# Attention in a two-layer block: two heads' values beside each other in the array, weight sums as strips of ones, queries for two pairs at a time

## The chip, the cores and the metric

The kernel runs on one core of a Trainium2 chip. A core has five engines that work side by side and meet through semaphores: TensorE (PE, matrix products, results in PSUM; its weight loads are listed apart as PEld), VectorE (DVE), ScalarE (ACT), GpSimd (POOL) and SyncE (SP, which here issues the transfers from memory). Each engine takes its instructions strictly in the order of the program. The metric is the device time of one execution in microseconds (us), lower is better.

## The reference

The reference is a block of two layers on 512 tokens of 1024 features, with 256 context tokens. Layer 0 mixes by Fourier and long convolution, layer 1 by attention with compressed queries and keys; each ends in a feed-forward network with a short convolution. The change lies in the attention of layer 1, of which this is the core (16 heads; a head has 64 plain and 32 rotated query features and 64 value features; keys are the 512 tokens and the 256 of the context):

```python
def _mla_queries(a_q, q_a_norm, w_uq, q_norm, rope):
    q = (_rms_norm(a_q, q_a_norm) @ w_uq).reshape(B, L, MLA_HEADS, QK_HEAD_DIM)
    q = _rms_norm(q, q_norm)
    ...
    s = jnp.einsum('bqhd,bkhd->bhqk', qblk, k, preferred_element_type=jnp.float32) * scale
    p = jax.nn.softmax(s, axis=-1).astype(v.dtype)
    return jnp.einsum('bhqk,bkhv->bqhv', p, v)
```

## The kernel before

Features lie on partitions and tokens along the free axis. Most products are done three times in float32r (`mm3`, lines 175 to 177): high part times high part, and the two cross terms with the low parts, which `hi` (line 150, ACT) and `lo` (line 155, DVE) split off. Products on plain fp32 operands are one call and appear as two records each.

The attention stage works on eight pairs of heads. It is written as small steps, each a function of a pair `p` and a few indices, and the text `ORDER` lists them with an offset: the loop runs through the list again and again, and a step with offset `o` is done for pair `it + o`. Inside `manual_schedule` this order is the order on PE, DVE, ACT and POOL. So it is a cyclic pipeline over pairs; steps that belong to only one pair (`only`) are left out in the other rounds. The steps, with the lines of their work:

- `QT` makes the queries of a pair (512 tokens x 192 features, 24 products of 192 columns, tile `k`), `SQ` squares them (ACT, L1521), `TB` and `TX` multiply by the rotation tables (DVE, L1526 and L1530), `RD` sums the squares (L1534).
- `UK` makes the pair's keys (tile `k`), `KSQ`, `KH`, `KL` square, copy and split them, `KS` sums the squares by twelve small records (L1557). `RT` takes the roots of queries and keys together: 13 small DVE instructions (L1562, L1563 and `rsqrt`, L184 to L193).
- `U` scales the queries (ACT, L1570), `TR` transposes them (PE, L1577), `QC` and `QL` copy and split them.
- `SC` makes the scores of head `a` with key tile `j` in one of three banks `s`: head 0 by `mm3`, head 1 by a fp32 product (L1597). `EV` brings them to `S`, scaled (ACT, L1605).
- `MA` to `MD` (DVE) and `AR` (POOL, L1623) find the maximum over the keys, `SU` subtracts it (DVE, L1627), `EX` takes the exponential (ACT, L1630).
- `VP` and `VE` make the values of all heads once, in `V`. There, for each pair, 64 columns of ones stand between the two heads' 64 value columns. `PW` (L1651) multiplies 128 columns of it, the values and the ones, by the weights of one head and one key tile: twelve fp32 products of full width a pair, in a bank `pv` for each head. Half of the result are the values, half are the sums of the weights, repeated over 64 rows.
- `TZ` (L1657) and `TO` (L1662) copy sums and values out (ACT, half the rows at a time), `RC` (L1666) takes the reciprocal of the sums over 256 columns twice, `DV` (L1680) divides, `OH` and `OL` split the result.
- `WO` are output products that belong to the next stage, of two of its eight row blocks; `WA`, `WD`, `XA`, `XD` load and split weights, the loads by SP.

A product in strips exists in this kernel too: in `gemv_pe` (L236, before the first layer) four products of 32 output columns each stand side by side in the array, in fp32 over 512 columns, each with its own moving operand.

## Time and profile before

| | us |
|---|---|
| median of 3 runs | 1598.99 (1595.99 to 1599.34) |
| the profiled execution | 1599.1 |
| its span | 1597.3 |
| PE busy in the span | 1561.7 |
| DVE busy | 1058.8 |
| ACT busy | 626.1 |
| POOL busy | 109.0 |

The span runs from the first to the last instruction of the profiled execution. Busy time of matmuls is modelled, since they are pipelined: the time between two starts says what one costs, not its own length. In the lines of the profile `L1651` is a line of the kernel, `pv<-S,V` names what is written from what, `x192` counts records, and the two numbers behind the bar are the total in us and the mean of one in ns; what follows is idle time before these instructions and what ended it. On the chain of waits a piece has its start, the time that it holds the chain, and its engine and line.

### The profile page before, as it was taken

How to read it: one execution, taken by the hardware profiler on the slowest of the kernel's cores; microseconds unless marked ns; L12 is line 12 of the kernel's file. 1: busy time of each engine (PE TensorE's matmuls, PEld its weight loads, DVE VectorE, ACT ScalarE, POOL GpSimd, SP SyncE). 2: the span in 40 equal slices, each digit the busy share in tenths (PEclk: the TensorE clock that was granted, in tenths of full speed). 3: DMA queues.
4: the chain of work that ended last, by engine and by line, in shares of the span. 5: the costliest groups of instructions: out<-in, count | busy, mean ns of one | idle time of the engine just before them, and what ended most of it. 6: DMA issues, size and time to landing. Idle time of an engine off the chain costs nothing.

```text
span 1597.3 us, 20872 instructions
## 1 busy us (share of the span) xinstructions
PE 1561.7 (98%) x8248; PEld 1291.2 (81%) x8248; DVE 1058.8 (66%) x1772; ACT 626.1 (39%) x909; POOL 109.0 (7%) x113
## 2 busy tenths in 40 slices
PE   7999999999999999999999999999999999999999
PEld 4787888888888888888888887566559888888887
DVE  5788969878986356653464577899987644344343
ACT  4451234434223113221132347898853432233231
POOL 0012135000000000000000000221210000000000
PEclk9999999999999999999999999999999999999999
DMA  9336412532543134431342310000033222222222
GB/s 351 107 115 211 175 48 87 185 119 107 184 151 140 64 135 158 166 111 66 113 168 82 111 50 1 14 11 14 0 110 141 93 93 96 103 93 96 102 80 92
DMA packets 54542, 173.36 MB, mean 109 GB/s; under 512 B 6187, under 2 KB 9453, under 8 KB 53421
## 3 DMA queue, kind: packets, MB, share of 16 engines
q1 hardware_dynamic: 54445, 172.03, 30.5%
q8 instruction: 65, 1.06, 0.3%
q14 instruction: 32, 0.26, 0.0%
HBM read 166.24 MB, written 5.77 MB: 108 GB/s over the span
## 4 chain that ended last, share of the span: by engine, by line
PE 79%; DVE 15%; ACT 2%; issue 2%; POOL 1%; DMA 1%; SPq 0%; POOLq 0%; DVEq 0%; ACTq 0%
PE mm L175 23%; PE mm L177 23%; PE mm L176 23%; PE pv L1651 2%; DVE junk L260 2%; DVE S L1627 2%; DVE wl L155 1%; PE s L1597 1%; DVE wr L1666 1%; DVE hl L330 1%; ACT wh L150 1%; PE ms L236 1%; PE mm L638 1%; DVE mx L1611 1%; DVE nt L325 0%
## 5 line engine op out<-in xcount | busy, mean ns | idle before, releaser
L150 ACT ACTIVATE wh<-wr 128x1024 fp32r<-128x1024 f32 (+1 forms) x192 | 198.3, 1035 | 548.2 <-PE mm L176 512.5
L175 PE MATMUL mm<-hh,wh 128*128 128x512 f32 (+1 forms) x872 | 339.9, 391 | 2.1 <-ACT hh L326 0.9
L176 PE MATMUL mm<-hl,wh 128*128 128x512 f32 (+1 forms) x872 | 338.4, 388 | 2.3 <-DVE hl L330 2.3
L177 PE MATMUL mm<-hh,wl 128*128 128x512 f32 (+1 forms) x872 | 338.2, 388 | 1.9 <-DVE wl L155 1.9
L155 DVE TENSOR_TENSOR wl<-wr,wh 128x1024 fp32r<-128x1024 f32 (+2 forms) x192 | 231.4, 1208 | 143.6 <-ACT wh L150 139.3
L177 PEld LDWEIGHTS mm<-hh,wl 128*128 128x128 f32 x872 | 165.2, 190 | 35.5 <-DVE wl L155 2.5
L175 PEld LDWEIGHTS mm<-hh,wh 128*128 128x128 f32 x872 | 165.2, 190 | 35.2 <-issue 2.9
L176 PEld LDWEIGHTS mm<-hl,wh 128*128 128x128 f32 x872 | 165.6, 190 | 32.6 <-DVE hl L330 3.5
L260 DVE SCALAR_TENSOR_TENSOR junk<-wr,sb 128x1024 bf16<-128x1024 f32 x128 | 156.1, 1220 | 47.3 <-DMA wr<-wmodT 47.1
L1171 DVE SCALAR_TENSOR_TENSOR xr<-mm,mod,xr 128x512 f32<-128x512 f32 (+1 forms) x100 | 61.8, 631 | 170.0 <-PE mm L177 169.7
L176 PE MATMUL mm<-hlc,wh 128*128 128x256 f32 (+1 forms) x488 | 137.6, 282 | 0.0
L175 PE MATMUL mm<-hhc,wh 128*128 128x256 f32 (+1 forms) x488 | 137.6, 282 | 0.0
L177 PE MATMUL mm<-hhc,wl 128*128 128x256 f32 (+1 forms) x488 | 137.4, 282 | 0.0
L176 PE MATMUL mm<-al,wh 128*128 128x512 f32 x328 | 127.8, 389 | 0.0
L177 PE MATMUL mm<-ah,wl 128*128 128x512 f32 x328 | 127.7, 389 | 0.0
L175 PE MATMUL mm<-ah,wh 128*128 128x512 f32 x328 | 127.7, 389 | 0.0
L1651 PE MATMUL pv<-S,V 128*128 128x512 f32 x192 | 93.9, 598 | 2.6 <-ACT S L1630 2.6
L175 PEld LDWEIGHTS mm<-hhc,wh 128*128 128x128 f32 x488 | 91.7, 188 | 3.9
L176 PEld LDWEIGHTS mm<-hlc,wh 128*128 128x128 f32 x488 | 91.7, 188 | 3.9
L177 PEld LDWEIGHTS mm<-hhc,wl 128*128 128x128 f32 x488 | 93.4, 191 | 0.0
L1214 DVE TENSOR_TENSOR fg<-fg,mm 128x768 f32<-128x768 f32 (+1 forms) x44 | 36.1, 821 | 76.4 <-PE mm L177 75.7
L1212 ACT ACTIVATE fg<-fg 128x768 f32<-128x768 f32 (+1 forms) x44 | 32.5, 739 | 123.9 <-DVE fg L395 94.4
(381 smaller groups left out, 2836.0 us busy)
## 6 DMA issues: line engine op xcount, KB each, us to landing
wr<-w_up SPq DMA_DIRECT2D x88, 512.0 KB, 3.2
wr<-wmodT SPq DMA_DIRECT2D x80, 512.0 KB, 3.2
wr<-w_dn SPq DMA_DIRECT2D x32, 512.0 KB, 3.1
wm<-wmod0a SPq DMA_DIRECT2D x8, 1024.0 KB, 9.7
wr<-w_in SPq DMA_DIRECT2D x16, 512.0 KB, 4.3
wr<-w_out SPq DMA_DIRECT2D x13, 512.0 KB, 3.7
wr<-w_dn SPq DMA_DIRECT2D x17, 384.0 KB, 2.9
wr<-w_o SPq DMA_DIRECT2D x11, 512.0 KB, 3.5
```

The costliest lines, as they stand in the source:

```text
L150: self.nc.scalar.activation(dst, src, AF.Copy)
L155: (eng or self.nc.vector).tensor_tensor(dst, src, hi.bitcast(F32), op=ALU.subtract)
L175: mmul(out, wh, xh, start=start, stop=False)
L176: mmul(out, wh, xl, start=False, stop=False)
L177: mmul(out, wl, xh, start=False, stop=stop)
L236: nc.tensor.matmul(ps[32 * q : 32 * q + 32, :], self.sT[:, kt, :], raw[:, 512 * kt : 512 * kt + 512], start=kt < 4, stop=kt >= 4, tile_pos ...
L260: nc.vector.scalar_tensor_tensor(junk, raw, 1.0, self.sb[:, j, :], op0=ALU.mult, op1=ALU.mult, accum_out=acc)
L1171: nc.vector.scalar_tensor_tensor(x[m][:, a2:b2], ps[:, a2 + o : b2 + o], mod[:, 8 * sec + m, c : c + 1], x[m][:, a2:b2], op0=ALU.mult, op1 ...
L1212: nc.scalar.activation(g[:, :n], g[:, :n], AF.Silu)
L1214: v.tensor_tensor(a[:, :n], g[:, :n], pss[1][:, :n], op=ALU.mult)
L1627: v.tensor_tensor(c.S[a][h], c.S[a][h], mb.to_broadcast([P, 3, T]), op=ALU.subtract)
L1651: nc.tensor.matmul(c.P[a], V[:, j, o : o + 128], c.S[a][j // 3][:, j % 3, :], start=j == 0, stop=j == 5)
```

## The change

The change rewrites the attention stage and nothing outside of it.

- Values: `V` holds 1024 columns without ones. `PW` for a key tile is two products of 64 columns, one for each head, placed by `tile_position` at columns 0 and 64 of the array; both heads share one bank.
- Weight sums: `ZS` sums the weights by products with 32 columns of ones, four of them (head, half of the key tiles) at columns 0, 32, 64 and 96 of the array, three steps a pair, in one bank. `ZT` transposes the bank in blocks of 32x32 on DVE, `ZM` adds the two halves of each head by a small fp32 product with a 0/1 matrix (`fold`), `ZR` takes the reciprocal of 16 columns, `ZB` spreads it by another transpose, `DV` multiplies the values straight out of PSUM. `TZ`, `TO` and `RC` go.
- Queries: `QT`, `SQ`, `TB`, `TX`, `RD` work on four heads and half of the tokens (products of 384 columns), and `RT` takes the roots of two pairs (40 columns); the first two pairs' roots are taken in two parts.
- Both heads keep the plain features on rows 0 to 63 and the rotated ones on 64 to 127, and the keys of both heads have two buffers; the second buffers' rotated rows are copied by POOL in `RX`. The fills of `V` with ones go.
- PSUM banks and the tiles `S` (seven instead of six) are handed out by `Ring` in the order of the list.
- `ORDER` is no longer a cycle: it names each step with its pair once, 658 of them, behind a short `OPENING`. For `QT`, `SQ`, `TB`, `TX`, `RD`, `RT`, `WA` and `WD` the number behind the colon is that of two pairs.

On PE the strip products of the list form these stretches (products of one strip width with no other product of PE between): pair 0 seven, then five, seven, five, seven, five, five and four, 45 in all; eleven of them follow directly on a stretch of the other width. In the diff, table and mask constants and the renamed indices are left out.

```diff
-SU01:-1 VE30:5 SC02:0 SC03:0 SC04:0 UK:1 OL:-3 EV02:0 XD0:1 RD:1 PW00:-1 VE40:1 AR1:-1 EV03:0 SU10:-1 EV04:0 VE51:-1 WO11:-2
...
+QT1:0 TB1:0 TX1:0 SQ1:0 RD1:0 WA:1 UK:0 KSQ:0 VP00:0 VE00:0 KH0:0 KL0:0 KH1:0 VP01:0 KS:0 VE01:0 UK:1 KSQ:1 KH0:1 RT0:0 VP10:0 VP20:0 VE20:0 VE10:0
...
+OH:3 PW2:4 RT2:3 MB0:5 U0:6 ZS0:4 TR0:6 QC0:6 SC11:5 ZS1:4 MC0:5 MD0:5 EV10:5 OL:3 U1:6 ZS2:4 SC14:5 QL0:6 EV11:5 SC13:5 EV13:5 SC12:5 SC00:6 ZT:4
+EV14:5 OL:2 U0:7 PW3:4 AR0:5 SC15:5 EV12:5 EV15:5 PW4:4 SU01:5 SC03:6 KH0:7 MA1:5 MB1:5 EX01:5 ZM:4 MC1:5 MD1:5 SU00:5 EV03:6 TR1:6 ZR:4 PW5:4 EV00:6
+SC01:6 ZB:4 KL0:7 QC1:6 EV01:6 SC04:6 SC02:6 EV04:6 SC10:6 EX00:5 AR1:5 EV10:6 SC11:6 EV11:6 SC05:6 EV02:6 EV05:6 DV:4 TR0:7 SC13:6 MA0:6 SU10:5
+SU11:5 EX10:5 MB0:6 SC12:6 PW0:5 EX11:5 MC0:6 PW1:5 ZS0:5 ZS1:5 U1:7 ZS2:5 QC0:7 EV12:6 PW2:5 SC14:6 EV13:6 EV14:6 MD0:6 TR1:7 PW3:5 OL:1 QL0:7 SC15:6
+ZT:5 QC1:7 SC02:7 EV15:6 KH1:7 SC00:7 AR0:6 SU00:6 MA1:6 MB1:6 EV00:7 SC01:7 OH:4 EV01:7 PW4:5 EV02:7 MC1:6 MD1:6 PW5:5 SC03:7 SU01:6 ZM:5 SC10:7
...
+AR0:7 WO03:7 MD1:7 PW4:6 SU00:7 WO04:7 AR1:7 ZT:6 ZM:6 PW5:6 ZR:6 ZB:6 WO11:7 DV:6 WO12:7 SU10:7 WO13:7 WO14:7 SU01:7 SU11:7 EX00:7 EX10:7 EX01:7
+EX11:7 PW0:7 OH:6 OL:5 PW1:7 PW2:7 OL:6 ZS0:7 ZS1:7 ZS2:7 PW3:7 PW4:7 ZT:7 ZM:7 ZR:7 PW5:7 ZB:7 WO15:7 WO16:7 WO05:7 DV:7 OH:7 WO06:7 OL:7 WO17:7
+WO07:7
 """
+OPENING = "QT0:0 RO:0 SQ0:0 TB0:0 TX0:0 RD0:0 RX:0"
...
+class Ring:
+    def __init__(self, tiles):
+        self.free = list(tiles)
+        self.left = {}
+
+    def get(self, uses):
+        t = self.free.pop(0)
+        self.left[id(t)] = uses
+        return t
+
+    def put(self, t):
+        self.left[id(t)] -= 1
+        if not self.left[id(t)]:
+            self.free.append(t)
+
...
-        K = [[self.t(pa, [P, TV], F32R if a in SPLIT else F32, f"K{a}{q}") for q in range(2)] for a in range(2)]
-        keys = lambda p, a: K[a] if a in SPLIT else [K[a][p % 2]]
+        K = [[[self.t(pa, [P, TV], F32R if a in SPLIT else F32, f"K{a}{r}{q}") for q in range(2 if a in SPLIT else 1)] for r in range(2)] for a in range(2)]
+        rot, ksel, fold = msk[0:64, 0:128], msk[:, 128:130], msk[:, 130:258]
...
-            K2 = lambda: self.t(psB, [P, 1024], F32, "k2", 1)
-            S1 = lambda: self.t(psB, [P, 512], F32, "s", 3)
+            K2 = self.ring(psB, [P, 1024], "k2", 1)
+            S1 = self.ring(psB, [P, 512], "s", 3)
+            MS = self.ring(psB, [P, 512], "ms", 1)
+            PV = self.ring(psB, [P, 512], "pv", 2)
...
-                        self.hi(K[a][0][rows, o : o + m], ps[rows, :m])
+                        self.hi(K[a][0][0][rows, o : o + m], ps[rows, :m])
-                    if a not in SPLIT:
-                        nc.gpsimd.tensor_copy(K[a][1][rows, :], K[a][0][rows, :])
+                            self.lo(K[a][0][1][rows, o : o + m], ps[rows, :m], K[a][0][0][rows, o : o + m])
+                    for k0, k1 in zip(*K[a]):
+                        nc.gpsimd.tensor_copy(k1[rows, :], k0[rows, :])
...
-            for j in range(6):
-                nc.gpsimd.memset(V[:, j, :].rearrange("p (a b) -> p a b", b=192)[:, :, 64:128], 1.0)
...
+            def QT(c, s, g):
+
+                ps = c.q[g] = K2.get(3)
+                wh, wl = wq[s]
+                for t_ in range(2):
                     for k in range(2):
+                        r, w = slice(256 * g + 128 * t_, 256 * g + 128 * t_ + 128), slice(384 * k, 384 * k + 384)
+                        self.mm3(ps[:, 512 * t_ : 512 * t_ + 384], qah[k][:, r], qal[k][:, r], wh[:, w], wl[:, w], k == 0, k == 1)
+
...
+            def SQ(c, s, g):
+                c.qs = self.t(pq, [P, TV], F32, "sq", 2)
+                nc.scalar.activation(c.qs.rearrange("p (t f) -> p t f", t=2), heads(c, g), AF.Square)
+                K2.put(c.q[g])
+
+            def TB(c, s, g):
+
+                if g == 0:
+                    c.t = self.t(pq, [P, 4, 4, 128], F32, "t2")
+                v.tensor_tensor(c.t[:, 2 * g : 2 * g + 2, :, 0:96], heads(c, g).rearrange("p t (a f) -> p t a f", a=4),
+                                tabm[:, 2 * g : 2 * g + 2, :].rearrange("p t (o f) -> p t o f", o=1).to_broadcast([P, 2, 4, 96]), op=ALU.mult)
+                K2.put(c.q[g])
+
+            def TX(c, s, g):
+                v.tensor_tensor(c.t[:, 2 * g : 2 * g + 2, :, 96:128], heads(c, g).rearrange("p t (a f) -> p t a f", a=4)[:, :, :, 64:96],
+                                tabx[:, 2 * g : 2 * g + 2, :].rearrange("p t (o f) -> p t o f", o=1).to_broadcast([P, 2, 4, 32]), op=ALU.mult)
+                K2.put(c.q[g])
+
+            def RD(c, s, g):
+                if g == 0:
+                    c.d = self.t(self.sm, [P, 24], F32, "rd_s")
+                v.tensor_reduce(c.d[:, 8 * g : 8 * g + 8], c.qs.rearrange("p (a f) -> p a f", a=8), AX.X, ALU.add)
 
...
             def KH(c, p, a):
-                rows = slice(0, 64) if a == 0 else slice(64, 128)
+                self.hi(K[a][p % 2][0][0:64, :], c.k[64 * a : 64 * a + 64, :TV])
+                K2.put(c.k)
...
-            def RT(c, p):
-
-                s = self.t(self.sm, [P, 24], F32, "nrm_s", 4)
-                v.tensor_scalar(s[:, 0:8], c.s[:, 0:8], 1.0 / 96, EPS, op0=ALU.mult, op1=ALU.add)
-                v.scalar_tensor_tensor(s[:, 8:20], c.rt[:, 0:12], 1.0 / 96, ssp[:, 8:20], op0=ALU.mult, op1=ALU.add)
-                c.r = self.t(pq, [P, 24], F32, "rks", 3)
-                self.rsqrt(self.sm, s, 20, c.r)
+                    o = 12 * c.i + 2 * j
+                    nc.tensor.matmul(c.s.rt[:, o : o + 2], c.ks[:, t0 : t0 + 128], ksel, start=True, stop=True)
+
+            def RT(c, s, m):
+
+                a, b = ((0, 28), (28, 40), (0, 40))[m]
+                x = self.t(pq, [P, 40], F32, "nrt_s", 2)
+                if a == 0:
+                    v.tensor_scalar(x[:, 0:16], c.d[:, 0:16], 1.0 / 96, EPS, op0=ALU.mult, op1=ALU.add)
+                    c.r = self.t(pq, [P, 40], F32, "rks", 2)
+                l = max(a, 16)
+                v.scalar_tensor_tensor(x[:, l:b], c.rt[:, l - 16 : b - 16], 1.0 / 96, ssp[:, l - 16 : b - 16], op0=ALU.mult, op1=ALU.add)
+                MS.put(c.rt)
+                self.rsqrt(pq, x[:, a:b], b - a, c.r[:, a:b], 40)
 
...
             def EV(c, p, a, j):
                 if j % 3 == 0:
-                    c.S[a].append(self.t(Sp, [P, 3, T], F32, "S"))
-                g = 8 + 2 * j + a
-                nc.scalar.activation(c.S[a][j // 3][:, j % 3, :], c.ps[a, j], AF.Copy, scale=c.r[:, g : g + 1])
+                    c.S[a, j // 3] = SS.get(6)
+                g = 16 + 12 * c.i + 2 * j + a
+                nc.scalar.activation(c.S[a, j // 3][:, j % 3, :], c.ps[a, j], AF.Copy, scale=c.s.r[:, g : g + 1])
+                S1.put(c.ps[a, j])
 
...
-            def PW(c, p, a, j):
+            def PW(c, p, j):
 
                 if j == 0:
-                    c.P[a] = PV()
-                o = 192 * p + 64 * a
-                nc.tensor.matmul(c.P[a], V[:, j, o : o + 128], c.S[a][j // 3][:, j % 3, :], start=j == 0, stop=j == 5)
-
-            def TZ(c, p, a):
-                if a == 0:
-                    c.zz = self.t(self.W, [P, 1024], F32, "wr")
-                    c.z = c.zz[:, 0:512]
-                nc.scalar.copy(c.z[64 * a : 64 * a + 64, :], c.P[a][64 - 64 * a : 128 - 64 * a, :])
-
-            def TO(c, p, a):
-                if a == 0:
-                    c.O = self.t(pq, [P, T], F32, "O", 2)
-                nc.scalar.copy(c.O[64 * a : 64 * a + 64, :], c.P[a][64 * a : 64 * a + 64, :])
-
-            def RC(c, p, h):
-                z = c.z[:, 256 * h : 256 * h + 256]
-                v.reciprocal(z, z)
+                    c.P = PV.get(1)
+                for a in range(2):
+                    o = 128 * p + 64 * a
+                    nc.tensor.matmul(c.P[64 * a : 64 * a + 64, :], V[:, j, o : o + 64], c.S[a, j // 3][:, j % 3, :], start=j == 0, stop=j == 5,
+                                     tile_position=(0, 64 * a))
+                    SS.put(c.S[a, j // 3])
+
+            def ZS(c, p, i):
+
+                if i == 0:
+                    c.zz = PV.get(1)
+                for a in range(2):
+                    for h in range(2):
+                        o = 64 * a + 32 * h
+                        nc.tensor.matmul(c.zz[o : o + 32, :], self.ones32, c.S[a, h][:, i, :], start=i == 0, stop=i == 2, tile_position=(0, o))
+                        SS.put(c.S[a, h])
 
             def ZT(c, p):
 
-                v.transpose(c.zz[:, 512:1024], c.z)
+                c.z = self.t(self.W, [P, 1024], F32, "wr")
+                v.transpose(c.z[:, 512:1024], c.zz)
+
+            def ZM(c, p):
+                nc.tensor.matmul(c.zz[:, 0:16], fold, c.z[:, 512:1024].rearrange("p (b c) -> p b c", c=32)[:, :, 0], start=True, stop=True)
 
             def ZR(c, p):
                 c.zr = self.t(pq, [P, 16], F32, "zr")
-                v.reciprocal(c.zr, c.zz[:, 512:1024].rearrange("p (b c) -> p b c", c=32)[:, :, 0])
+                v.reciprocal(c.zr, c.zz[:, 0:16])
+                PV.put(c.zz)
 
             def ZB(c, p):
-                v.transpose(c.z, c.zr.rearrange("p (b o) -> p b o", o=1).to_broadcast([P, 16, 32]))
+                v.transpose(c.z[:, 0:512], c.zr.rearrange("p (b o) -> p b o", o=1).to_broadcast([P, 16, 32]))
 
             def DV(c, p):
-                v.tensor_tensor(c.O, c.O, c.z, op=ALU.mult)
+                c.O = c.z[:, 512:1024]
+                v.tensor_tensor(c.O, c.P, c.z[:, 0:512], op=ALU.mult)
+                PV.put(c.P)
 
...
+            by_two = ("QT", "SQ", "TB", "TX", "RD", "RT", "WA", "WD")
+
+            def run(order):
+                for token in order.split():
+                    name, p = token.split(":")
+                    f, p = name.rstrip("0123456789"), int(p)
+                    args = [int(n) for n in name[len(f):]]
+                    ops[f]((two if f in by_two else pairs)[p], p, *args)
+
+            run(OPENING)
             self.dbg("lat", kvh, kvl, qah, qal)
             self.close("pt")
```

More of the change, by code (lines that the diff above doesn't have):

```diff
@@ L187, in rsqrt @@
         for step in range(3):
-            a = self.t(pool, [P, 24], F32, "rq_a")
+            a = tile_("rq_a")
             v.tensor_tensor(a[:, :n], r, r, op=ALU.mult)
-            b = self.t(pool, [P, 24], F32, "rq_b")
+            b = tile_("rq_b")
             v.scalar_tensor_tensor(b[:, :n], a[:, :n], -0.5, s[:, :n], op0=ALU.mult, op1=ALU.mult)
-            r2 = out if step == 2 and out is not None else self.t(pool, [P, 24], F32, "rq_r")
+            r2 = out if step == 2 and out is not None else tile_("rq_r")
             v.scalar_tensor_tensor(r2[:, :n], b[:, :n], 1.5, r, op0=ALU.add, op1=ALU.mult)
@@ L1502, in attention @@
             class Pair:
                 pass
[L1505 removed]
+            pairs, two = [Pair() for _ in range(KD)], [Pair() for _ in range(KD // 2)]
+            for p, c in enumerate(pairs):
+                c.s, c.i = two[p // 2], p % 2
+                c.qT, c.ps, c.S, c.m, c.vp = {}, {}, {}, {}, {}
+            for c in two:
+                c.q = {}
             wo = {}
[L1509 to L1513 removed]
+            def QT(c, s, g):
+                ps = c.q[g] = K2.get(3)
+                wh, wl = wq[s]
+                for t_ in range(2):
@@ L1739, in attention @@
             Oh = [self.t(pO, [P, T], F32R, f"Oh{p}") for p in range(KD)]
-            Sp = self.pool("Sp", bufs=6)
-            for it in range(-max(s[2] for s in steps), KD - min(s[2] for s in steps)):
-                for f, args, off in steps:
-                    p = it + off
-                    if 0 <= p < KD and p in only.get(f, (p,)) and (p or f not in done):
-                        ops[f](pairs[p], p, *args)
+            Sp = self.pool("Sp")
+            SS = self.ring(Sp, [P, 3, T], "S", 7)
+            run(ORDER)
         self.dbg("V", V)
@@ L1955, in layouts @@
     uq = mla_w_uq[0].reshape(2, P, 16, 96)
-    heads = [uq[:, :, h, :] if h % 2 == 0 else np.concatenate([uq[:, :, h, 64:], uq[:, :, h, :64]], -1) for h in range(16)]
-    uq = np.stack(heads).reshape(4, 2, 2, 2, P, 96)
-    r["w_uq"] = uq.transpose(0, 4, 1, 3, 2, 5).reshape(4, P, 768)
+    r["w_uq"] = uq.reshape(2, P, 4, 4, 96).transpose(2, 1, 0, 3, 4).reshape(4, P, 768)
     ukv = mla_w_ukv[0].reshape(P, 16, 128)
```

199 lines of the change are left out of this document (90 added, 109 removed).

## The prediction

> **What bounds the kernel now.** I read the page first, then the chain of waits, then the busy time by windows, the waits of PE, and the groups of one stage. The change touches only the attention stage, so its window decides.
>
> ```profile
> 960.00:1192.00 232.00, 228.53 (x912) 143.69 (x912) 207.25 (x290) 190.92 (x299) 46.06 (x17) 0.99 0.05 16
> ```
>
> Columns: length, then busy time of PE, PEld, DVE, ACT, POOL. The stage runs from 960 to 1192 us; PE is called busy for 228.5 of 232 us, but ends of matmuls are modelled, so I check this by the chain:
>
> ```profile
> 1023.03 0.86 PE pv L1651 x2
> ...
> 1042.89 0.44 PE s L1577 x4
> 1043.33 0.86 PE s L1597 x2
> ...
> 1047.21 0.23 PE s L175
> ...
> 1052.25 0.12 PE k L175
> ...
> 1057.59 1.23 PE ms L1557 x12
> ...
> 1068.47 0.45 PE s L1577 x4
> 1068.95 0.61 ACT q L150
> 1069.58 0.69 DVE ql L155
> ```
>
> The columns are start, length on the chain, engine and line. From the transposes of one pair (1042.89) to those of the next (1068.47) are 25.58 us, and in them the chain never leaves PE. On the chain a fp32 product of 128x512 is two records of 0.43 us; a float32r product of 512 columns takes 0.23, of 256 columns 0.12. Twelve small records take 1.23 us. After 1068 it runs over DVE, and this row shows why:
>
> ```profile
> 1042.89:1068.47 25.58, 25.58 (x107) 15.97 (x105) 24.86 (x35) 23.25 (x37) 6.11 (x3) 1.00 0.00 1
> 1094.00:1119.50 25.50, 25.50 (x106) 15.88 (x105) 25.03 (x35) 22.32 (x36) 6.35 (x3) 1.00 0.04 14
> ```
>
> ```profile
> PE pv L1651 <- ACT S L1630: 2.6, 4, 1.0
> PE pv L175 <- ACT V L1642: 0.5, 1, 0.5
> PE k L176 <- DVE Ol L155: 0.2, 1, 0.2
> ```
>
> A pair takes 25.5 us; DVE has up to 25.0 us of work in it and ACT 22.3. The last three rows are all that PE waited for in the stage: 3.3 us. So PE is the bound with DVE half a microsecond behind. A change pays only if it relieves both, and then by the smaller relief. The granted clock is 1.00 in these rows, so slots can be compared.
>
> **The change part by part: PE.** Counts come from these rows of the stage:
>
> ```profile
> L1651 PE MATMUL pv<-S,V 128*128 128x512 f32 x192 | 93.9, 598 | 2.6 <-ACT S L1630 2.6
> ...
> L175 PE MATMUL k<-wh,qah 128*128 128x192 f32 x56 | 17.6, 314 | 0.0
> ```
>
> *Values.* 192 records in slots of 0.43 us are 82.6 us. Afterwards the two heads' products of one key tile are 64 columns wide each and stand side by side in the array. No row shows 64 columns; the nearest is the modulation's product in four strips of 32 columns:
>
> ```profile
> 44.42 0.28 PE L177 MATMUL mm<-hhc,wl 128*128 128x260 f32 x1
> 44.63 1.92 PE L236 MATMUL ms<-wm,sT 128*32 128x512 f32 x16
> 46.48 0.50 PE L175 MATMUL mm<-hh,wh 128*128 128x512 f32 x1
> ```
>
> Sixteen fp32 records over 512 columns, each strip with a moving operand of its own, take 46.48 - 44.63 = 1.85 us, while sixteen slots of 0.43 would be 6.9. Four strips thus run together, in 4 x 0.43 = 1.72. Two strips of 64 should do the same: 192 records in 96 slots, 41.3 us, a gain of 41.3. The bounds are this and no overlap at all (gain 0); I take the first, since the row differs only in width.
>
> *Weight sums.* New: three steps a pair, each four 32-column strips, two passes: 8 x 3 x 2 x 0.43 = 20.6 us, directly by that row (without overlap 82.6).
>
> *Queries.* Half as many products, of 384 instead of 192 columns. [...]
>
> ```profile
> 1064.23 0.27 PE L175 MATMUL k<-wh,qah 128*128 128x192 f32 x1
> 1064.34 0.27 PE L176 MATMUL k<-wl,qah 128*128 128x192 f32 x1
> ```
>
> They start 0.11 apart. 384 columns cost 3/4 of 0.23 = 0.17. So 192 x 0.11 = 21.1 becomes 96 x 0.17 = 16.5: a gain of 4.6.
>
> *The small product that folds the strips.* 16 records of 1.23/12 = 0.10: 1.6 us.
>
> *Changing the width of the strips.* In the three rows above, the 260-column product started at 44.42 has a slot of 0.12 and so ends its slot at 44.54; the strips start 0.09 later, and after them the next product starts 0.13 after 44.63 + 1.72. One excursion costs 0.22 us. In the written order I count 45 stretches of strip products, 11 of which follow directly on one of the other width: 34 excursions and 11 inner changes, 34 x 0.22 + 11 x 0.11 = 8.7 us. Bounds: 0 (the weights could be loaded as early as for full products) and, if the array ran empty at each change, the record's length less its slot, 0.598 - 0.43 = 0.17 each way: 34 x 0.34 + 11 x 0.17 = 13.4. I take 8.7, the measured one.
>
> [...]
>
> Sum for PE: -41.3 + 20.6 - 4.6 + 1.6 + 8.7 = -15.0 us, or 1.9 us a pair, from 25.5 to 23.6. It ranges from -23.7 (changes free) to -10.3.
>
> **DVE and ACT** must follow.
>
> ```profile
> L1627 DVE TENSOR_TENSOR S<-S,mx 128x1536 f32<-128x1536 f32 x32 | 55.3, 1749 | 2.3 <-POOL mx L1623 2.3
> L1666 DVE RECIPROCAL wr<-wr 128x256 f32<-128x256 f32 x16 | 27.5, 1735 | 0.0
> ...
> L1680 DVE TENSOR_TENSOR O<-O,wr 128x512 f32<-128x512 f32 x8 | 5.5, 682 | 0.2
> ...
> L1644 DVE COPY V<-pv 128x512 f32<-128x512 f32 x6 | 4.1, 691 | 2.8 <-PE pv L177 2.7
> ```
>
> ```profile
> 1060.44 0.15 DVE L1562 TENSOR_SCALAR nrm_s<-rd_s 128x8 f32<-128x8 f32 x1
> ...
> 1062.82 0.18 DVE L193 SCALAR_TENSOR_TENSOR rks<-rq_b,rq_r 128x20 f32<-128x20 f32 x1
> ```
>
> The two long reciprocals go (3.47 us a pair). In come two 32x32-block transposes over 512 columns, a reciprocal of 16 columns, and a product that reads PSUM. The trace has no transpose on DVE; from below a copy of 512 columns out of PSUM takes 0.69, from above a reciprocal at 1.735 per 256 would make it 3.5. Moving data is nearer to the copy: 0.7 each. The short reciprocal lies between the 0.18 of the last row and 0.3; I take 0.25. The product costs the same from PSUM (0.69 against 0.68). The roots run from 1060.44 to 1063.00, 2.56 us for a pair; done for two pairs at once, with 40 instead of 20 columns, they save about 1.2 a pair. DVE: -3.47 + 1.65 - 1.2 = -3.0 us a pair, 25.0 to 22.0. That is below PE's 23.6, so PE stays the bound. At the dear end of the transposes DVE would need 27.6, dealt with as a rival. The squares, tables and reductions of the queries move the same number of elements in the same number of instructions.
>
> [...]
>
> ```profile
> L1662 ACT COPY O<-pv 64x512 f32<-64x512 f32 x16 | 9.3, 581 | 0.4
> L1657 ACT COPY wr<-pv 64x512 f32<-64x512 f32 x16 | 9.3, 579 | 0.3
> ...
> L1521 ACT ACTIVATE sq<-k 128x768 f32<-128x768 f32 x8 | 6.4, 805 | 0.7 <-PE k L177 0.7
> ```
>
> ACT loses the four half copies, 2.3 us a pair (22.3 to 20.0). The bank of the values is now held until DVE's product, but the list puts that product before the next pair needs the bank.
>
> **Waits, moves, transfers.** The fold product waits on PE for DVE's transpose; behind it in PE's order stand scores of later pairs. In the middle of the stage the list has eight products between the last strip sum and the fold (pair 4: six of two 0.43 slots, two of three 0.23), 6.5 us, so I cost the wait at nothing; uncovered it costs the transpose plus one subtraction that may be running on DVE, 0.7 + 1.75 = 2.4 us a pair. At the head the evictions of scores decide, taken alone in this row of ACT up to the first values:
>
> ```profile
> 960.00:1001.20 41.20, 9.38 (x15) 0.96 0.00 1
> ```
>
> The old order had 15 evictions behind it when the values began; the list has 18, and a third pass over the queries, ahead of them. Three evictions and that pass are 3 x 0.63 + 0.8 = 2.7 us more on ACT; I add 2 us of PE idling, between 0 (other products fill it) and 5 (the second pair's score tail is in the way as well). For what else moves:
>
> ```profile
> L1500 POOL MEMSET V<- 128x512 f32 x6 | 2.9, 524 | 685.7 <-PE mm L177 685.7
> L1496 POOL COPY K<-K 64x768 f32<-64x768 f32 x1 | 0.8, 816 | 8.8 <-ACT K L150 8.8
> ...
> wr<-w_o SPq DMA_DIRECT2D x11, 512.0 KB, 3.5
> wr<-w_uq SPq DMA_DIRECT2D x4, 384.0 KB, 3.0
> ```
>
> Pieces of w_uq and w_o are issued earlier on SP's queue, which moves 16 GB/s in the stage and lands a piece in 3 to 3.5 us: nothing. Six POOL fills go and two copies of 0.8 us come, in the opening, needed only by the second pair's scores; POOL has 186 of 232 us free: nothing. At the stage's end the reciprocal leaves the chain, but output products cover it anyway:
>
> ```profile
> 1182.23 0.80 PE L175 MATMUL k<-Oh,wh 128*128 128x512 f32 x1
> ...
> 1189.40 0.40 PE L177 MATMUL k<-Oh,wl 128*128 128x512 f32 x1
> ```
>
> They fill PE from 1182.2 to 1189.8 while the last pair's reciprocals run, so I count nothing there.
>
> The profiled execution took 1599.1 us (span 1597.3 and 1.8 around it), 0.1 from the median of the runs, 1598.99. Sum: 1599.0 - 15.0 + 2.0 = **1586.0 us**. With both ends of the width changes and of the head's wait: 1575 (changes free, no wait) to 1594 (full drains, 5 us of wait).
>
> **The rivals.**
> *Width changes cost nothing.* For it: between fp32 and float32r products the chain shows no gap at all (0.23 follows 0.86). Against: the gap of 0.22 in the strips' rows. PE saves 23.7, DVE's 22.0 is then level with PE's 22.5; with the head's wait 1577.
>
> *The order gives it back.* Once PE needs 23.6, DVE 22.0 and ACT 20.0, every in-order wait counts, and the old cyclic order let PE wait 3.3 us in all. If the folds stand uncovered in six pairs or so (6 x 2.4 = 14), nothing is left: 1600, in a band from 1595 to 1605.
>
> *Strips of 64 columns do not overlap (the slower side).* If the second head's product runs behind the first, the values take 82.6 us as before and the sums come on top: -15.0 + 41.3 = +26.3, so 1627 with the head's 2. The point from which it decides: as soon as the strips hide less than about 70% of each other (13 of 41.3 us eaten), the gain is gone. For it: no row shows this width. Against: four narrower ones do overlap fully. This is also the case in which the change does not do what it says.
>
> *Dear transposes.* At 3.5 us each DVE needs 27.6 a pair, 2.1 above the present period: 1599 + 17 = 1616.
>
> **How the numbers follow.** Forecast 0.54 (its own range 1578 to 1594), free changes 0.16, the order gives it back 0.16, no overlap 0.10, dear transposes 0.04. The range 1573 to 1603 leaves out the last two and the tails of others, some 0.18. What a measurement can tell from no change is 0.2%, 3.2 us, so faster means under 1595.8: forecast, free changes and a little of the third, 0.74. Within: half of the third, 0.08. Slower: 0.18.
>
> **What would show it.** Right: value records in pairs starting together, slots of 0.43; the strip sums in groups of four; a pair period near 23.6 with PE still without gaps; transposes near 0.7 us; no reciprocal of 256 columns. Wrong: a second strip starting 0.43 behind the first; gaps on PE released by the transpose, by evictions on ACT, or at each change of width larger than 0.2; DVE with no idle time; a period at 25 or above.

## The result and the profile after

| | before | after |
|---|---|---|
| time, median of 12 runs each (us) | 1599.16 (1595.99 to 1603.56) | 1597.12 (1594.06 to 1601.19) |
| ratio after / before, 95% interval | | 0.9988 (0.9977 to 0.9999) |
| profiled execution: time, span (us) | 1599.1, 1597.3 | 1596.66, 1594.9 |
| the attention stage in it (us) | 960.07 to 1191.75: 231.7 | 956.29 to 1187.75: 231.5 |
| from there to the start of the last product with the attention's outputs, `mm<-Oh,wl` (us) | 33.7 | 35.3 |

The forecast was 1586.0; the kernel became 0.12% faster, which is less than the 0.2% that the prediction took as the least that can be told from no change. The stage is measured on the chain of waits, from the first product of ones with the squares of the rotary keys to the first product of the sweep with w_o behind it. It hardly shrank: 0.2 us. The execution began it 3.8 us sooner and lost 1.6 us behind it. Of the 3.8 us, 0.6 are the first queries, which stand ahead of the stage and take 2.3 us instead of 2.8; for the rest, this start lies between 956.2 and 962.6 us in the kernel after and those below, though all but e_q192 have the same work ahead of it, so it may be scatter.

First the windows of the kernel before: the whole stage, its first 60 us (the head) and all that stands behind them. Columns: length, busy time of PE, PEld, DVE, ACT and POOL, then the granted clock, the DMA share and GB/s.

```profile
960.07:1191.75 231.68, 228.21 (x909) 143.37 (x909) 207.18 (x290) 190.67 (x298) 46.06 (x17) 0.99 0.04 16
960.07:1020.10 60.03, 58.35 (x282) 41.79 (x282) 44.18 (x86) 47.42 (x83) 8.39 (x4) 0.97 0.00 1
1020.10:1191.75 171.65, 169.85 (x628) 101.58 (x627) 163.00 (x205) 143.25 (x216) 37.66 (x13) 1.00 0.06 21
```

The same three of the kernel after:

```profile
956.29:1187.75 231.46, 224.74 (x1032) 121.99 (x1033) 178.96 (x259) 171.80 (x266) 37.33 (x19) 0.98 0.05 18
956.29:1016.30 60.01, 55.31 (x248) 39.98 (x250) 42.54 (x85) 45.32 (x78) 7.81 (x6) 0.91 0.00 1
1016.30:1187.75 171.45, 169.44 (x786) 82.01 (x787) 136.41 (x174) 126.49 (x190) 29.52 (x13) 1.00 0.07 24
```

DVE's work in the stage fell by 28.2 us and ACT's by 18.9; behind the head DVE is busy for 80% of the time, where it was for 95%. Nothing of that shows in the time. PE is called busy for nearly all of it, so the question is what fills PE. The groups of the changed products and of DVE's new instructions, kernel after (busy us, mean ns, idle before):

```profile
L1710 PE MATMUL pv<-S,V 128*64 128x512 f32 x192 | 50.8, 610 | 0.4 <-ACT S L1690 0.3
L1721 PE MATMUL pv<-S,ones 128*32 128x512 f32 x192 | 24.3, 599 | 0.0
L1727 DVE STREAM_TRANSPOSE wr<-pv 128x512 f32<-128x512 f32 x8 | 5.7, 709 | 4.0 <-PE pv L1721 4.0
L1738 DVE STREAM_TRANSPOSE wr<-zr 128x512 f32<-128x512 f32 x8 | 5.7, 708 | 0.2
L1742 DVE TENSOR_TENSOR wr<-pv,wr 128x512 f32<-128x512 f32 x8 | 5.5, 683 | 0.4
L1734 DVE RECIPROCAL zr<-pv 128x16 f32<-128x16 f32 x8 | 2.0, 255 | 8.9 <-PE pv L1730 8.9
```

and its chain of waits over two runs of strips (start, length, line):

```profile
1153.31 2.58 PE s L1659 x6
1155.88 2.73 PE pv L1710 x12
1158.61 2.71 PE pv L1721 x24
1161.32 1.06 PE s L1659 x2
```

Twelve value records, three steps of two strips with two passes each, take 2.73 us: six slots of 0.43 and 0.15 more. Twenty-four sum records, three steps of four strips, take 2.71: again six slots, and 0.13. So strips of 64 columns run side by side in full, and what is left over is the price of changing the width. The two full products behind them hold the chain for 1.06 instead of 0.86; what of that belongs to the change is worked out below.

That gives an account of PE. Each record in the stage is priced at the undisturbed slot of its kind (0.43 us for a fp32 record of 512 columns, half and a quarter of it for a strip of 64 and of 32, 0.23 for a float32r product, 0.17 and 0.11 for the queries' 384 and 192 columns):

| us of the stage | before | after | difference |
|---|---|---|---|
| sum of slots | 223.8 | 201.0 | -22.8 |
| changes of width: 34 excursions, 11 inner changes | 0 | 13.0 | +13.0 |
| the rest: PE idle, at a lower clock, or late without being called idle | 7.9 | 17.5 | +9.6 |
| stage | 231.7 | 231.5 | -0.2 |

The slots shrank as forecast. Two other rows ate it: the first is priced from the strips below, the second is what remains and is looked at next.

**Where a change of width is paid.** Kernel after, timeline of PE (start, length, line, operation, shape):

```profile
1116.06 1.02 PE L1659 MATMUL s<-q,K 128*128 128x512 f32 x2
1117.02 1.92 PE L1721 MATMUL pv<-S,ones 128*32 128x512 f32 x16
1118.87 2.41 PE L1659 MATMUL s<-q,K 128*128 128x512 f32 x5
```

Two records from 1116.06 would end their slots at 1116.92; the strips begin 0.10 later. Sixteen strip records are four slots, 1.71, to 1118.73; the scores begin 0.14 later. The third part hides in the first full product after the strips, and the kernel before has it at the modulation's strips:

```profile
46.48 0.50 PE L175 MATMUL mm<-hh,wh 128*128 128x512 f32 x1
46.82 0.40 PE L176 MATMUL mm<-hl,wh 128*128 128x512 f32 x1
47.06 0.39 PE L177 MATMUL mm<-hh,wl 128*128 128x512 f32 x1
```

The product started at 46.48 holds PE for 0.34 us, the next one for 0.24. That is 0.10 more. So 0.10 + 0.14 + 0.10 = 0.34 for one excursion; a change between strips of 64 and 32 costs 0.13. With 34 and 11 of them: 11.6 + 1.4 = 13.0. The kernel after shows the third part too: a fp32 score product that starts right behind strips holds PE for 0.53 us instead of 0.43, at all 16 such places of the stage.

A smaller number of columns does not cost this by itself. The kernel before has float32r products of 64 columns that are not placed by `tile_position`, and between a full product and these PE keeps its slots:

```profile
945.28 0.28 PE L177 MATMUL mm<-hhc,wl 128*128 128x256 f32 x1
945.40 0.39 PE L175 MATMUL mm<-hh,whpe 128*64 128x512 f32 x1
945.63 0.39 PE L176 MATMUL mm<-hl,whpe 128*64 128x512 f32 x1
```

The last full product takes 0.12, the first narrow one 0.23, both as usual. So "change of width" here always means the change to or from strips placed side by side.

**Where the rest lies.** PE's waits in the stage, kernel after (total, times, longest):

```profile
PE k L216 <- ACT sq L1571: 2.9, 2, 2.3
PE k L216 <- ACT K L191: 1.1, 2, 0.6
PE ms L1617 <- ACT sq L1600: 0.7, 1, 0.7
PE k L216 <- DVE K L196: 0.7, 1, 0.7
PE k L216 <- DVE t L1583: 0.6, 1, 0.6
PE s L216 <- ACT S L1665: 0.3, 1, 0.3
PE pv L1710 <- ACT S L1690: 0.3, 1, 0.3
```

Of these 6.6 us, 5.3 are products into the one k2 buffer (queries and key rows) that wait for its last readers on ACT and DVE. The largest stands in the head:

```profile
961.17 0.34 PE L218 MATMUL k<-wh,qal 128*128 128x384 f32 x1
963.80 0.79 PE L216 MATMUL k<-kvh,wh 128*128 128x512 f32 x1 [2.29 <-ACT sq L1571]
964.39 0.63 PE L217 MATMUL k<-kvl,wh 128*128 128x512 f32 x1
964.82 0.63 PE L218 MATMUL k<-kvh,wl 128*128 128x512 f32 x1
```

The key rows of the first pair wait 2.3 us for the squares of the second half of the queries, which read the same bank. Behind the wait a float32r product holds PE for 0.43 us instead of 0.23, at a granted clock of 0.50. The trace of after has three such stretches of 3.41 us at 0.50 in the stage, at 964, 970 and 1008 us, all in the head; before had one, at 962. Only the first of the three follows a wait of this size: ahead of the other two PE had idled for 0.6 and 0.7 us. By the windows the head has 4.7 us of PE idle at a mean clock of 0.91, before 1.7 at 0.97: 3.0 us of idling, and two more stretches at half clock, 2 x 3.41 / 2 = 3.4 us. That is 6.4 of the 9.6 us. Behind the head the profile calls PE idle for 2.0 us, but it did so for 1.8 us in the kernel before as well (1020.10 to 1191.75). The other 3 us are no idle time by the profile. By the starts of the records they too lie behind the head: there PE falls 6.7 us behind its slots and width changes, where it fell 3.6 behind in the kernel before. Which waits these are is not shown.

### The profile page after: what moved, and what is told of

It reads as the page before. It is cut to its first block, busy times and chain, and to the rows that moved or that the text cites. A ratio compares the mean times of both kernels' runs of the same rounds, so it can differ in the third digit from the quotient of the medians.

```text
span 1594.9 us, 21009 instructions
## 1 busy us (share of the span) xinstructions
PE 1556.0 (98%) x8360; PEld 1267.6 (79%) x8360; DVE 1029.9 (65%) x1740; ACT 607.9 (38%) x877; POOL 97.3 (6%) x109
## 4 chain that ended last, share of the span: by engine, by line
PE 83%; DVE 11%; ACT 2%; issue 1%; DMA 1%; POOL 1%; SPq 0%; ACTq 0%; DVEq 0%; POOLq 0%
PE mm L216 23%; PE mm L218 23%; PE mm L217 23%; PE pv L1710 3%; PE s L1659 3%; DVE junk L301 2%; DVE wl L196 1%; PE pv L1721 1%; PE s L216 1%; PE k L216 1%; PE k L218 1%; PE k L217 1%; DVE hl L371 1%; PE s L218 1%; PE s L217 1%
## 5 line engine op out<-in xcount | busy, mean ns | idle before, releaser
L216 PEld LDWEIGHTS mm<-hh,wh 128*128 128x128 f32 x872 | 164.6, 189 | 35.1 <-issue 2.9
L218 PEld LDWEIGHTS mm<-ah,wl 128*128 128x128 f32 x328 | 61.6, 188 | 12.8
```

The lines of the kernel that those rows point to most:

```text
L216: mmul(out, wh, xh, start=start, stop=False)
L218: mmul(out, wl, xh, start=False, stop=stop)
```

## The experiments

Two theories were set against each other. A: TensorE's own stream is the bound, an excursion costs 0.34 us, and the stage is the sum of slots, width changes and a head. B: the time is set by in-order waits for ScalarE and VectorE, and PE's stream only fills what they leave. Each kernel was compared with the kernel before on the same chip. "Rest" below is the stage less the slots and the width changes, as in the table above. A stage is that of the one profiled execution of its kernel, the time is the median of all its runs; what lies outside of the stage took between 1362 and 1371 us in these executions.

**Strips gathered by the order.** Only the written order is edited; shown is PE's order for pair 4.

```
- after:   PW0 PW1 SC10 PW2 ZS0 TR0 SC11 ZS1 ZS2 SC14 SC13 SC12 SC00 PW3 SC15 PW4 SC03 ZM TR1 PW5
+ e_two:   PW0 PW1 PW2 ZS0 ZS1 ZS2 SC14 SC13 SC12 SC00 SC15 PW3 PW4 PW5
+ e_one:   ZS0 ZS1 ZS2 PW0 PW1 PW2 PW3 PW4 PW5
+ e_split: PW0 SC10 PW1 PW2 TR0 ZS0 SC11 ZS1 SC14 ZS2 SC13 SC12 SC00 PW3 SC15 PW4 SC03 ZM TR1 PW5
```

> Only the order of PE's strip products is changed: of each pair, the first three value products and the three strip sums stand in a row, and the other three value products in a row. 15 excursions to strips and 9 inner changes of width instead of 34 and 11. Theory A (each excursion costs PE 0.34 us, an inner change 0.13, and PE is the bound): 19 x 0.34 + 2 x 0.13 = 6.7 us less than the changed kernel, about 1590. Theory B (PE's time is set by waits for ACT and DVE in the written order, the changes of width lie in these waits): within 2 us of the changed kernel, or slower, since scores come later.

> All nine strip steps of a pair stand in a row, sums first: 8 excursions and 8 inner changes. Theory A: 26 x 0.34 + 3 x 0.13 = 9.2 us less than the changed kernel, about 1588, less what ACT loses while PE makes no scores for 7.7 us. Theory B: no gain, slower by some us because evictions on ACT run dry during the block.

> The opposite: neighbouring strip steps are pulled apart by the next full product: 51 excursions and 5 inner changes. Theory A: 17 x 0.34 - 6 x 0.13 = 5.0 us more than the changed kernel, about 1602. Theory B: within 2 us of it.

| kernel | excursions, inner changes | width changes (us) | rest (us) | stage (us) | time (us) | ratio to before |
|---|---|---|---|---|---|---|
| after | 34, 11 | 13.0 | 17.5 | 231.5 | 1597.12 | 0.9988 (0.9977 to 0.9999) |
| e_two | 15, 9 | 6.3 | 38.1 | 245.4 | 1609.13 | 1.0069 (1.0047 to 1.0091) |
| e_one | 8, 8 | 3.8 | 55.9 | 260.6 | 1625.99 | 1.0169 (1.0144 to 1.0194) |
| e_split | 51, 5 | 18.0 | 20.6 | 239.6 | 1609.03 | 1.0067 (1.0046 to 1.0087) |

Fewer excursions made it slower, and so did more. The strips in a row save 6.7 and 9.2 us of width changes and lose 20.6 and 38.4 elsewhere, so A's 1590 and 1588 us were missed by far. PE's waits in the stage of e_one:

```profile
PE pv L1721 <- ACT S L1690: 7.2, 7, 2.8
PE s L216 <- ACT S L1665: 5.8, 8, 1.6
PE k L216 <- DVE t L1583: 3.2, 3, 1.9
PE k L216 <- ACT sq L1571: 2.8, 2, 2.3
```

The gathered strips wait for the last exponentials (L1690), and then the scores of the next pair wait for evictions (L1665), which came late in turn. The clock is lower too; two windows of e_one from its middle:

```profile
1040.00:1080.00 40.00, 35.23 (x175) 17.94 (x176) 27.74 (x43) 26.12 (x39) 5.35 (x3) 0.96 0.00 0
1080.00:1120.00 40.00, 34.57 (x142) 16.95 (x139) 27.54 (x31) 25.35 (x39) 5.94 (x2) 0.96 0.04 14
```

PE idles 5 us of 40, and the clock is 0.96, where the kernel after has 1.00 behind its head. These three cannot separate the theories: an order that saves changes makes waits. e_split does go A's way, but further: 8.1 us more of stage for 5.0 expected, and a time of 1609.03 where A said about 1602.

**The head.** In e_head the second half of the queries, with its squares and rotations, and the first two values' projections are put ahead of the rotary outputs; no arithmetic changes.

```
-OPENING = "QT0:0 RO:0 SQ0:0 TB0:0 TX0:0 RD0:0 RX:0"
+OPENING = "QT0:0 RO:0 SQ0:0 TB0:0 TX0:0 QT1:0 SQ1:0 TB1:0 TX1:0 RD0:0 VP00:0 VP01:0 RX:0"
```

> Only the head of the list is changed: the second half of the first queries is squared on ACT before the rotated key rows are copied, and two products of the values stand on PE before the first keys. In the changed kernel PE waits 2.3 us there for these squares, and its clock is halved three times for 3.4 us in the first 60 us of the stage. Theory A: 2 to 4 us less than the changed kernel. Theory B (the head is hidden by later slack): within 1 us.

It took 1598.75 us, 1.0010 (0.9994 to 1.0026) of before, with a stage of 232.3. Neither theory gave that: A wanted 2 to 4 us less than the kernel after and B a time within 1 us of it, and by the ratios it lies 3.5 us above. The wait at the key rows went, and one of 3.1 us came at the sums of the keys' squares:

```profile
PE ms L1616 <- ACT sq L1599: 3.8, 2, 3.1
```

Behind it PE's slots were doubled, as in the stretches at half clock of the kernel after: from 968.7 to 974.4 us (2.72 for the twelve small records instead of 1.23, 0.43 for a float32r product instead of 0.23), and once more from 1008.7 to 1011.4 (0.43 again). This one way of moving the same work did not fill the head.

**The same order without strips.** Here the order and every step's slot stay, and only the width changes go. The kernels of this part leave out a part of the values or sums; in e_full and in e_zs1 below, the short reciprocal is an addition of 1.

```
-                for a in range(2):
-                    o = 128 * p + 64 * a
-                    nc.tensor.matmul(c.P[64 * a : 64 * a + 64, :], V[:, j, o : o + 64], c.S[a, j // 3][:, j % 3, :], start=j == 0, stop=j == 5,
-                                     tile_position=(0, 64 * a))
+                nc.tensor.matmul(c.P, V[:, j, 128 * p : 128 * p + 128], c.S[j % 2, j // 3][:, j % 3, :], start=j == 0, stop=j == 5)
...
-                        nc.tensor.matmul(c.zz[o : o + 32, :], self.ones32, c.S[a, h][:, i, :], start=i == 0, stop=i == 2, tile_position=(0, o))
+                nc.tensor.matmul(c.zz, self.ones32[:, 0:1].to_broadcast([P, P]), c.S[int(i > 0), int(i > 1)][:, i, :], start=i == 0, stop=i == 2)
```

e_full has both edits, e_fullpw the first alone.

> No strips at all, at the changed kernel's own order: each value step is one product of 128 columns (head 0 for even key tiles, head 1 for odd ones), each sum step one product of 128 columns of ones over one tile of weights; half of the values and three quarters of the sums are left out, and the short reciprocal is an addition of 1 so that no zero sum is inverted. The slots of the steps stay (0.86 us each), only the changes of strip width go. Theory A (TensorE's own stream is the bound; each of the 34 excursions costs 0.34 us and each of the 11 inner changes 0.13): stage 231.5 - 13.0 = 218.5 us, time about 1584. Theory B (waits for ScalarE and VectorE in the written order set the stage; the time saved turns into longer waits): stage 228 to 232, time 1594 to 1597.

> Only the value steps are full-width products (half of the values left out); the sums keep their four strips. 13 excursions and no inner change stay of 34 and 11. Theory A: 231.5 - (13.0 - 4.4) = 222.9 us of stage, time about 1588.5. Theory B: stage 229 to 232, time 1595 to 1597.

| kernel | excursions, inner changes | width changes (us) | rest (us) | stage (us) | time (us) | ratio to before |
|---|---|---|---|---|---|---|
| e_full | 0, 0 | 0 | 17.4 | 218.4 | 1583.84 | 0.9908 (0.9896 to 0.9921) |
| e_fullpw | 13, 0 | 4.4 | 19.2 | 224.6 | 1590.57 | 0.9945 (0.9931 to 0.9958) |

In e_full the stage is 218.4 us against A's 218.5, and the time 1583.84 against 1584. e_fullpw lies 1.7 us above A's stage; its profiled execution was the slowest of five, at a mean granted clock of 0.988 where the other four had 0.990 to 0.992. The window of e_full, in the columns of before:

```profile
957.10:1175.50 218.40, 210.17 (x794) 133.55 (x794) 178.63 (x259) 171.23 (x266) 37.29 (x19) 0.98 0.05 16
```

DVE and ACT do the same work as in the kernel after (178.63 and 171.23 us against 178.96 and 171.80) and do it in 13 us less. So they were not the bound. The rest stays at 17.4 us: the width changes are an addition of their own, not a part of the waits. The full products also wait for fewer weights than the strips did, those of one head and tile at a time. That is not where the 13 us come from: in the kernel after, the value and sum products waited only 0.3 us for exponentials by its list of waits, and PE idles no less in e_full (8.2 us) than there (6.7).

**Less and more work on PE, same order.** e_zs1 keeps only the last of the three sum steps; e_q192 cuts the queries' products back to 192 columns.

```
-                        nc.tensor.matmul(c.zz[o : o + 32, :], self.ones32, c.S[a, h][:, i, :], start=i == 0, stop=i == 2, tile_position=(0, o))
+                        if i == 2:
+                            nc.tensor.matmul(c.zz[o : o + 32, :], self.ones32, c.S[a, h][:, i, :], start=True, stop=True, tile_position=(0, o))
...
-                        self.mm3(ps[:, 512 * t_ : 512 * t_ + 384], qah[k][:, r], qal[k][:, r], wh[:, w], wl[:, w], k == 0, k == 1)
+                            w = slice(384 * k + u, 384 * k + u + 192)
+                            self.mm3(ps[:, o + u : o + u + 192], qah[k][:, r], qal[k][:, r], wh[:, w], wl[:, w], k == 0, k == 1)
```

> Of the three sum steps of a pair only the last is kept (two thirds of the weights are not summed), and the short reciprocal is an addition of 1. 16 steps of 0.86 us go, with them 1 excursion and 4 inner changes: 14.6 us of TensorE's stream. Theory A: stage 217, time about 1582.5. Theory B: the order's later instructions wait for ScalarE and VectorE instead: stage 226 or more, time 1592 or more.

> The queries' products of 384 columns are cut in two of 192 again (everything is computed). 96 products of 0.174 us become 192 of 0.111: +4.6 us of TensorE's stream, a quarter of it in the head. Theory A: stage 236, time about 1601.7. Theory B: the longer stream fills waits that are there anyway: +2 us or less, time below 1599.5.

e_zs1 took 1584.84 us, 0.9909 (0.9895 to 0.9923) of before, with a stage of 217.5 against A's 217 and B's 226:

```profile
956.70:1174.20 217.50, 210.01 (x906) 117.93 (x906) 177.93 (x259) 170.86 (x266) 37.29 (x19) 0.98 0.05 17
```

e_q192 took 1603.28 us, 1.0025 (1.0015 to 1.0035). Against the kernel after the ratio rises by 0.0037, or 5.9 us, where A gave 4.6 and B at most 2. Its stage is 234.5, 3.0 us more; A's 236 counted all the queries, though 0.6 us of the 4.6 lie ahead of the stage. So PE's stream is paid about one for one both ways: 14.0 us of stage for 14.6 of stream, 3.0 for 4.0. B falls as long as the order stays.

**What comes behind the stage.** In e_tail low parts of outputs move up, so that buffers come free sooner for pieces of w_o: that of pair 4 by 44 tokens, that of pair 5 by 58; pair 6's already stood there and changes places with one strip step.

```
- OH:4 EV01:7 PW4:5 EV02:7 MC1:6
+ OH:4 EV01:7 PW4:5 EV02:7 OL:4 MC1:6
...
- OH:5 SU10:6 SC05:7 EV04:7 EV05:7
+ OH:5 SU10:6 SC05:7 EV04:7 OL:5 EV05:7
```

> Only the low parts of the outputs of pairs 4, 5 and 6 are moved up, to four steps behind their high parts, so that the buffers of the ring shared with the weight pieces come free sooner. If the late pieces of w_o behind the stage cost the 1.5 us by which the part after it grew, that part shrinks from 35.3 to 33.8 us and the time from 1597.1 to about 1595.6; if those pieces are covered, the time stays within 0.5 us of 1597.1. The stage itself stays at 231.5 by both theories.

It took 1597.45 us, 1.0002 (0.9990 to 1.0015), with a stage of 233.3, which both theories had left at 231.5. The part behind the stage is 35.1 us against 35.3. The chains of waits there, of the kernel after

```profile
1184.27 1.23 DVE wl L196
1185.51 6.87 DMA wr<-w_o
1192.46 1.07 ACT wh L191
```

and of e_tail

```profile
1189.12 1.23 DVE wl L195
1190.37 6.20 DMA wr<-w_o
1196.65 1.07 ACT wh L190
```

The piece starts 4.9 us later, as the whole end of the stage does (1192.6 against 1187.75), and still behind a low part of weights on DVE. The low parts of the outputs were not what held it. In kernels without any edit there this part takes from 34.4 us (e_q192) to 36.2 (e_zs1), all above the 33.7 of the one trace of before. So some of the 1.6 us may be scatter; that stays open.

**A gentler order.** e_merge1 has e_tail's edit, and at nine places the strips go behind the one full step that parted them from the next strips; e_best also lets four groups that wait for the k2 buffer go one score later. PE's order again:

```
- after:    PW0 PW1 SC10 PW2 ZS0 TR0 SC11 ZS1 ZS2 SC14 SC13 SC12 SC00 PW3 SC15 PW4 SC03 ZM TR1 PW5
+ e_merge1: PW0 PW1 PW2 ZS0 TR0 SC11 ZS1 ZS2 SC14 SC13 SC12 SC00 SC15 PW3 PW4 SC03 ZM TR1 PW5
...
- after:    KS:2 UK:3 SC02:1
+ e_best:   KS:2 SC02:1 UK:3
```

> The moved low parts, and beside them nine value or sum steps delayed past the one full-width step that separates them from the next strips: 25 excursions and 13 inner changes instead of 34 and 11. Theory A (each change is paid in full where no wait is made): stage 231.5 - 2.8 = 228.7 us, time 1.5 to 4.5 us below the changed kernel's, 1592.6 to 1595.6. Theory B (later strips free the buffers of weights later, and the evictions behind them make TensorE wait, as in the kernels with strips in long rows): stage 231.5 or more, time not below 1596.

> As the kernel with nine merged steps, and four full-width groups that wait 0.7 to 0.8 us for their bank (key rows of pairs 2, 3 and 5, second half of the queries of two pairs) go one score step later. Theory A (these waits are short and lie in front of TensorE's stream): another 1.5 to 3 us less than with the merged steps alone, stage 226 to 227, time about 1591. Theory B: the groups' own followers on ScalarE and VectorE are late in turn, stage unchanged against the merged steps or longer.

e_merge1 took 1601.87 us, 1.0026 (1.0014 to 1.0037), e_best 1605.49, 1.0044 (1.0026 to 1.0062). Their stages are 235.2 and 237.9 us: 2.8 us of width changes saved, 6.5 and 9.2 of rest added. PE's timeline in e_merge1 shows one of the places:

```profile
1043.93 0.66 PE L215 MATMUL k<-wh,qah 128*128 128x384 f32 x1 [1.94 <-ACT S L1689]
1044.38 0.52 PE L216 MATMUL k<-wl,qah 128*128 128x384 f32 x1
1044.70 0.52 PE L217 MATMUL k<-wh,qal 128*128 128x384 f32 x1
...
1046.88 0.34 PE L215 MATMUL k<-wh,qah 128*128 128x384 f32 x1
1047.05 0.34 PE L216 MATMUL k<-wl,qah 128*128 128x384 f32 x1
1047.23 0.34 PE L217 MATMUL k<-wh,qal 128*128 128x384 f32 x1
```

PE idles 1.94 us for an exponential, and then its products of 384 columns start 0.32 apart instead of 0.17: nine of them last from 1043.93 to 1046.88, 2.95 us where 9 x 0.174 = 1.57. The wait and the slower products behind it take 3.3 us together. Here B's sentence holds: evictions and exponentials behind the moved steps came late. No order that was tried beats the kernel after, and only kernels that leave work out do.

## Why the prediction was wrong

The mechanism was right, and the forecast missed by 11.1 us because two terms were mis-sized, the width changes and the head, and PE's waits behind the head were left out.

*Values, sums, queries, fold: right.* The forecast took 23.7 us of slots off; 22.8 went in the stage and 0.6 ahead of it. That two strips of 64 columns share the array was taken from four of 32, and they do, in full. The prediction's "No row shows 64 columns" misses the 128*64 products at 945.40 us, but these do not stand side by side and could not have settled it. By e_q192 the wider queries are worth 3.0 us of the stage or 5.9 of the time, on both sides of the 4.6 given to them. The rivals "no overlap" and "dear transposes" are out: a transpose takes 0.709 us, for which 0.7 was said, the short reciprocal 0.255 (0.25).

*DVE and ACT: right.* 28.2 and 18.9 us over eight pairs are 3.5 and 2.4 a pair, forecast 3.0 and 2.3. They left the bound, as e_full's window shows.

*"One excursion costs 0.22 us": mis-sized.* It costs 0.34, the sum 13.0 and not 8.7. The rows quoted for it already began with the product at 46.48, but its own slot, 0.34 to the next start at 46.82, was not read. The upper bound of 13.4, which supposed that the array runs empty at each change, came closest, though partly by luck: it has 0.17 each way, where 0.10 on the way to the strips and 0.24 behind them were measured. That the array runs empty was the author's supposition, in the full drains of the range too, and no run shows it; the runs show 0.34 us for a way out and back. The rival "width changes cost nothing" is refuted by e_full: they cost 13.1 us of stage.

*"I add 2 us of PE idling" in the head: too small and in the wrong place.* It was put at the evictions ahead of the first values. What came was a wait of the first key rows for the one k2 buffer, which the second half of the queries now holds, and two more stretches at half clock: 3.0 us of idling and 3.4 of clock, 6.4 in all, above the bound of 5. The forecast priced idle time alone and had no term for the clock, which was at 0.50 for 3.41 us three times, with slots of 0.43 for 0.23. The first of these stretches came with a wait of 2.3 us, those at 970 and 1008 us had 0.6 and 0.7 us of idling ahead of them; what sets one off is not shown.

*Behind the head: waits costed at nothing.* The fold's wait on PE was rightly taken as covered: no fold (L1730) stands in the list of waits. But PE falls 3.1 us further behind its slots there than in the old order (6.7 for 3.6), of which the profile calls only 0.2 idle; what it waits for stays open. The rival "the order gives it back" has the right time, 1595 to 1605, by another mechanism than its folds, so by luck.

*What lies around the stage.* The earlier start gives 3.8 us and the part behind it takes 1.6; but for the 0.6 us of the first queries, neither is shown to come from the change.

By the terms as measured: 1599.1 - 22.8 + 13.0 + 9.6 - 3.8 + 1.6 = 1596.7, the profiled execution's 1596.66. The 9.6 are what the other terms leave of the stage, so this sum has to come out; that 13.0 is right is shown by e_full. Of the miss, 4.3 us are width changes (13.0 for 8.7), 7.6 are waits and clock (9.6 for 2), 0.9 are slots; 2.2 came back around the stage, and 0.4 lies between that execution and the median.

## What to carry to other kernels

Count how often the array changes between full products and strips, and price one way out and back from the start of the last full product to the end of the first full product's slot behind the strips, not to its start: here 0.34 us each, so that 34 of them took more than half of what sharing the array had won. Gathering such steps did not mend this full order in any of four tries: strips moved later free buffers later, and at one place TensorE lost 3.3 us, 1.9 by a wait and 1.4 by slower products behind it. To learn what really bounds a stage, change the work and keep the order (full products in place of strips, or steps left out); a changed order answers a different question.

## What the runs showed of the hardware

- An excursion to strips is paid in three places: about 0.10 us before the strips, 0.14 behind them, and 0.10 in the slot of the first full product. Without strips the stage is 13.1 us shorter at the same order, 13.0 by the sum. A product of 64 columns that is not placed beside another costs no such change (0.12 and 0.23 us at 945.28 and 945.40).
- Two fp32 strips of 64 columns share the array with no loss: 12 records in 2.73 us, 0.15 of it the change.
- The granted clock falls to 0.50 for 3.41 us, sometimes 6.83 (after, from 243.36 us), and in the traces of before and after the falls start whole multiples of 3.41 us apart (after: 963.57, 970.40, 1007.95). In the 3.41 us ahead of these three PE had idled for 2.06, 0.55 and 0.68 us, and not at all ahead of the one at 962.34 in the kernel before; so a wait much shorter than 3.41 us can stand ahead of a fall, and so can no wait. In e_merge1 products of 0.17 us took 0.32 behind a wait of 1.94. Behind the head of the kernel after, with 2.0 us of waits in 171, the clock was 1.00.
